# A third shuffle buffer, attention products 28 chunks behind the scores, and the gate product behind later halves

## The chip, the cores and the metric

The kernel runs on one core of a Trainium2 chip. The metric is the device time of one execution in microseconds (us). Five engines run their own instruction streams in order and wait for each other by semaphores: TensorE (PE, matmuls; its weight loads are listed as PEld), VectorE (DVE), ScalarE (ACT), GpSimd (POOL) and SyncE (SP), which here issues every DMA.

## What is computed

One block of a diffusion backbone: a modulated RMS norm, one input projection, then two parallel branches (latent attention with 4 heads, and a multi-scale pooling), gates, an output projection and the residual. The change touches the attention alone. Cut to it:

```python
def _attend(q, k, v):                     # 4 heads, 2048 queries, 2304 keys
    s = einsum('bhqd,bhkd->bhqk', q, k) * scale
    p = softmax(s, axis=-1)
    return einsum('bhqk,bhkd->bhqd', p, v)

def _branches(u, mla_out, w_pool, pool_scale):
    br_a = silu(gate_a) * mla_out          # the gate that the change moves
    br_p = silu(gate_p) * _multiscale_pool(...)
    return concatenate([br_a, br_p], -1)
```

The kernel attends in the space of the 128 compressed values ("latents") and applies each head's value matrix afterwards; numerators are normalised only at the end, by the reciprocal sums of the softmax folded into the gate.

## The kernel before

The first 520 us hold the projections. Attention runs from about 520 to 1086 us, and the output projection from there to the end. The change lies in the attention.

**Tiling.** There are 16 blocks of 512 queries (4 heads by 4), and each block is two pairs of 128-query tiles; `p` counts the pairs, 0 to 31, and `i` the tile in a pair. The keys come in chunks: four of 512 columns and one of 256 for each tile, so a pair has 10 chunks (`PER`). Chunk 4 or 9 of a pair is the narrow one.

**Scores.** `scores(p, i)` makes a chunk with 5 fp16 matmuls (L772), takes its maximum on DVE (L775), and, once the five maxima of a tile are there, their bias on DVE (L780, L781). Then ACT takes the five exponentials (L793), and DVE transposes each in 32x32 blocks into a W buffer (L796). Wide chunks use the five PSUM banks pA, narrow ones the two banks pX. The pX banks also serve `norm` (L876) and `finish` (L903).

**Shuffle.** `shuffle(p)` moves the pair's transposed numerators with 16 DMAs (L811) from its transpose buffer (two, by p % 2) to a shuffled buffer (two, by p % 2), so that keys lie on partitions.

**Products with the latents.** `pv(p)` takes nine steps. Each step splits 512 shuffled columns into two fp16 halves, the high half on ACT (L853) and the low half on POOL, for step 4 on DVE (L855); then 6 matmuls (L821) add into one PSUM bank pO, two with the high half first, then four for which the low half must be there. Three buffers hold halves, so the halves of a step wait for the matmuls three steps back. One bank pO serves a block (two pairs); when it is full, `latents` splits it into two parts (ACT L96, DVE L97), and only then can the next block write pO.

**Gate.** `norm(n)` makes the reciprocal sums of a block (DVE L873, L874), turns them on PE (L876), copies them (DVE L878), sends them to DRAM (SP L879, L881), reads them back on all partitions (L884), loads the gate (L886), and multiplies both on POOL (L887). `finish` multiplies the latents by the head's value matrix (PE L903) and by the gate (DVE L905) and stores the result (SP L908).

**Order.** `attn` yields chunk by chunk and draws steps of `pv_all` by `while done < (gc - LAG) * 9 / PER`, with `LAG = 22` chunks. A list scheduler then fixes each engine's instruction order at compile time from these priorities, so an instruction can stand some places from where the source has it. `K_PF` loads the next head's keys behind pairs 3 and 5 of a head (L712), and `WO_PF` loads output weights behind pairs 28 to 30.

Of the kernel before, what the change touches and what calls it, by code (L numbers as in the profile page):

```python
# [12 lines left out]
ALU = mybir.AluOpType  # L13
# [39 lines left out]
ATT_MAX = 18  # L53


LAG = 22
K_PF = (3, 5)
WO_AT = (1, 5, 11, 12, 12, 12, 13, 13)
CHUNKS = ((0, 512), (512, 512), (1024, 512), (1536, 512), (2048, 256))
# [4 lines left out]
def tile_hybrid_block(ctx: ExitStack, tc: tile.TileContext, x, c, cx, c_ctx, w_mod, b_mod, norm_g,  # L64
                      w_in, q_lora_g, w_uq, kv_lora_g, w_ukv, q_norm_g, k_norm_g, w_pool,
                      pool_scale, w_out, rope_t, edge_t, out):
    nc = tc.nc
    x, cx, out = x[0], cx[0], out[0]
# [671 lines left out]
    tbuf, pbuf = [], []  # L740
# [57 lines left out]
        RS.setdefault(p // 2, []).append(rs)  # L798
        yield

    PT = {}

    def shuffle(p):

        src = TP.pop(p)
        if p < 2:
            pbuf.append(st("W", [4, 2, NJ, 32]))
        dst = pbuf[p % 2]
        for iq in range(4):
            for jq in range(4):  # L810
                last = nc.sync.dma_start(out=dst[32 * jq:32 * jq + 32, iq], in_=src[32 * iq:32 * iq + 32, jq])  # L811
        PT[p] = dst
        return last.ins
# [31 lines left out]
    def pv(p):  # L845
        o = out_bank(p)
        src = PT.pop(p).rearrange("p q i j b -> p (q i) j b")
        ts = []

        def halves(j2):  # L850
            t = st("M", [2, 2, 8, 32], F16)
            s2 = src[:, :, 2 * j2:2 * j2 + 2, :].rearrange("p x j b -> p j x b")
            nc.scalar.activation(out=t[:, 0], in_=s2, func=AF.Copy)  # L853
            eng = nc.vector if j2 == 4 or (p == NP - 2 and j2 % 2) else nc.gpsimd
            eng.tensor_tensor(out=t[:, 1], in0=s2, in1=t[:, 0], op=ALU.subtract)  # L855
            ts.append(t)

        for j2 in range(NJ // 2):
            if j2 == 0:
                halves(0)  # L860
                halves(1)
            if j2 + 2 < NJ // 2:
                halves(j2 + 2)
            t = ts.pop(0)
            pv_mm(p, o, j2, t)
            yield

    def norm(n):

        h, qb = blocks[n]  # L870
        s4 = small(4, "s4")
        for i in range(4):
            nc.vector.reduce_sum(s4[:, i:i + 1], RS[n][i], axis=AX.X)  # L873
        nc.vector.reciprocal(out=s4, in_=s4)  # L874
        b = pt("X")
        nc.tensor.transpose(b[0:4, 0:128], s4, ident)  # L876
        rr = sm.tile([4, 128], F32, tag="rr", bufs=2, name=nm("rr"))
        nc.vector.tensor_copy(out=rr, in_=b[0:4, 0:128])  # L878
        nc.sync.dma_start(out=rvd[n].rearrange("(s n i r) -> s i n r", s=2, n=4, i=2)[0],  # L879
                          in_=rr[0:2].rearrange("i (n r) -> i n r", n=4))  # L880
        nc.sync.dma_start(out=rvd[n].rearrange("(s n i r) -> s i n r", s=2, n=4, i=2)[1],  # L881
                          in_=rr[2:4].rearrange("i (n r) -> i n r", n=4))
        rb = st("T", [512])
        nc.sync.dma_start(out=rb, in_=rvd[n].partition_broadcast(128))  # L884
        ga = st("T", [512])
        nc.sync.dma_start(out=ga, in_=gad[h, :, qb * 512:(qb + 1) * 512])  # L886
        nc.gpsimd.tensor_tensor(out=ga.rearrange("p (r n) -> p r n", n=16),  # L887
                                in0=ga.rearrange("p (r n) -> p r n", n=16),
                                in1=rb.rearrange("p (n r) -> p r n", n=16), op=ALU.mult)
        return ga  # L890

    def latents(n):

        o = O.pop(n)
        ol = [st("T", [512], F32R) for _ in range(2)]
        split(o, *ol)
        return ol
# [31 lines left out]
    def pv_all():  # L929
        ol = None  # L930
        for p in range(NP - 2):
            if p % 2:
                gau = norm(p // 2)
            for k, _ in enumerate(pv(p)):
                if k == 2 and ol:
                    finish(p // 2 - 1, ol, gaus)
                    ol = None
                yield
            if p % 2:
                ol, gaus = latents(p // 2), gau  # L940
        gau = norm(NP // 2 - 1)
        for k, _ in enumerate(pv_last(NP - 1)):
            if k == 2:
                finish(NP // 2 - 2, ol, gaus)
            yield
        yield from pv(NP - 2)
        finish(NP // 2 - 1, latents(NP // 2 - 1), gau)

    PER = 10
# [3 lines left out]
    def attn():  # L953

        done = 0
        for p in range(NP):
            if p % 2 == 0 and p // 2 + 1 < len(blocks):
                load_q(blocks[p // 2 + 1])
            gc = p * PER
            h = p // 8 + 1  # L960
            for i in range(2):
                for _ in scores(p, i):
                    gc += 1
                    while done < (gc - LAG) * 9 / PER:
                        next(pg)
                        done += 1
                    yield
            if p == NP - 1:
                load_wo(3)
                return  # L970
            with tc.issue_after(shuffle(p)):
                if h < H and p % 8 in K_PF:
                    load_k(h, (K_PF.index(p % 8),))
                if p in WO_PF:
                    load_wo(WO_PF.index(p))
# [129 lines left out]
```

## Time and profile before

| | before |
|---|---|
| times of 3 runs | 1288.63, 1289.40 (median), 1295.37 us |
| the profiled execution | 1288.46 us, of which the span from first to last instruction is 1286.7 us |
| PE busy | 1212.8 us (94%) |
| DVE, ACT, POOL busy | 831.1 (65%), 738.5 (57%), 562.1 us (44%) |
| PE busy in 560 to 1086 us | 495.5 of 526 us |
| DVE, ACT, POOL busy in 560 to 1086 us | 422.6, 383.5, 300.9 us |
| mean granted TensorE clock | 0.984 of full speed |

"Busy" is the time in which an engine had an instruction running. A busy PE is not a PE at its peak: at the lower of its two clocks (1.2 instead of 2.4 GHz) the same matmuls are busy for twice as long. Times inside the profile count from the first instruction. The profile's time lies 0.94 us under the median of the runs.

### The profile page before, as it was taken

What the parts mean: (1) busy time and instruction counts of PE and PEld (TensorE: products, weight loads), DVE (VectorE), ACT (ScalarE), POOL (GpSimd) and SP (SyncE); (2) the same over time, 40 slices, a digit from 0 to 9 for tenths busy, and PEclk for the clock granted to TensorE, in tenths of its full rate; (3) what the DMA queues carried; (4) which work ended last, traced back from release to release, by engine and by line L of the source; (5) the groups of instructions that cost most, each with busy time, mean ns of one, the idle gap of its engine ahead of it and who ended that gap; (6) DMA issues with size and microseconds to landing.
All of it is one profiled execution on the core that took longest, in us unless ns stands there. A gap on an engine that the chain in (4) does not pass through costs nothing.

```text
span 1286.7 us, 22292 instructions
## 1 busy us (share of the span) xinstructions
PE 1212.8 (94%) x7805; PEld 954.5 (74%) x7805; DVE 831.1 (65%) x1595; ACT 738.5 (57%) x1780; POOL 562.1 (44%) x638
## 2 busy tenths in 40 slices
PE   6799999999999998988999989999899999899998
PEld 3698989989899998755566655666556667688887
DVE  4966654765666555677788887888778887631211
ACT  5575665655575654466777767777667777511000
POOL 3645313524344342025566645654656654332221
PEclk9799999999999999999999999999999999999999
DMA  9446952574446547367877787777777778563321
GB/s 304 149 122 138 228 137 66 130 198 136 94 108 153 113 126 196 90 150 172 199 188 181 182 203 188 182 176 196 185 176 183 179 191 236 194 238 135 115 98 49
DMA packets 208213, 208.66 MB, mean 162 GB/s; under 512 B 92339, under 2 KB 168420, under 8 KB 207974
## 3 DMA queue, kind: packets, MB, share of 16 engines
q1 hardware_dynamic: 208102, 207.25, 62.0%
q8 instruction: 61, 1.00, 0.3%
q14 instruction: 50, 0.41, 0.1%
HBM read 98.50 MB, written 35.56 MB: 104 GB/s over the span
## 4 chain that ended last, share of the span: by engine, by line
PE 70%; DMA 11%; DVE 5%; SPq 5%; ACT 4%; issue 2%; POOL 2%; ACTq 0%; DVEq 0%; POOLq 0%
PE pA L588 17%; PE pA L1028 14%; PE pA L772 14%; PE pO L821 9%; PE pA L244 6%; SPq L811 3%; PE pA L519 2%; POOL M L855 2%; DMA M<-in_w_in_dram 2%; DMA rvd<-rr 2%; ACT M L853 2%; PE pX L772 1%; DMA W<-W 1%; DVE W L796 1%; PE pA L494 1%
## 5 line engine op out<-in xcount | busy, mean ns | idle before, releaser
L855 POOL TENSOR_TENSOR M<-W,M 128x512 f16<-128x512 f32 x244 | 291.3, 1218 | 193.3 <-ACT M L853 193.2
L772 PE MATMUL pA<-B,M 128*128 128x512 f16 x1280 | 303.9, 381 | 7.0 <-ACT T L793 3.6
L588 PE MATMUL pA<-W,B 128*128 128x256 f32 x2304 | 307.3, 287 | 0.1
L588 PEld LDWEIGHTS pA<-W,B 128*128 128x128 f32 x2304 | 290.2, 192 | 3.5 <-issue 0.9
L772 PEld LDWEIGHTS <-M 128*128 128x128 f16 x1600 | 156.4, 98 | 145.6 <-issue 7.3
L821 PE MATMUL pO<-M,B 128*128 128x256 f16 x1728 | 222.1, 276 | 21.2 <-POOL M L855 20.3
L793 ACT ACTIVATE T<-pA,nm,gm 128x512 f32<-128x512 f32 x248 | 189.6, 775 | 62.7 <-DVE nm L781 62.7
L821 PEld LDWEIGHTS <-B 128*128 128x128 f16 x1728 | 168.9, 99 | 71.6 <-issue 31.6
L796 DVE STREAM_TRANSPOSE W<-T 128x512 f32<-128x512 f32 x310 | 197.6, 647 | 25.2 <-ACT T L793 14.3
L853 ACT ACTIVATE M<-W 128x512 f16<-128x512 f32 x279 | 164.7, 632 | 84.3 <-PE pO L821 65.2
L775 DVE TENSOR_REDUCE mx<-pA 128x1 f32<-128x512 f32 x256 | 173.3, 680 | 37.8 <-PE pA L772 36.3
L1028 PE MATMUL pA<-W,B 128*128 128x512 f32 (+1 forms) x792 | 178.7, 386 | 4.8 <-ACT B L96 4.8
L1028 PEld LDWEIGHTS pA<-W,B 128*128 128x128 f32 x792 | 146.0, 189 | 34.2 <-ACT B L96 5.1
L1052 POOL TENSOR_TENSOR M<-T,M 128x512 f32<-128x512 f32 x30 | 38.7, 1294 | 113.6 <-DVE T L1049 109.4
L1049 DVE TENSOR_TENSOR T<-pA,M 128x512 f32<-128x512 f32 (+1 forms) x33 | 22.0, 673 | 101.1 <-PE pA L1028 101.1
L244 PE MATMUL pA<-B,W 128*128 128x448 f32 (+1 forms) x288 | 86.4, 371 | 0.0
L97 DVE TENSOR_TENSOR B<-M,B 128x1024 fp32r<-128x1024 f32 x48 | 61.5, 1282 | 32.1 <-ACT B L96 32.0
L96 ACT ACTIVATE B<-M 128x1024 fp32r<-128x1024 f32 (+2 forms) x53 | 55.3, 1044 | 45.2 <-DMA M<-in_w_in_dram 37.5
L887 POOL TENSOR_TENSOR T<-T,T 128x512 f32<-128x512 f32 x16 | 24.6, 1540 | 82.8 <-DMA T<-gad 49.5
L96 ACT ACTIVATE B<-B 128x2048 fp32r<-128x2048 f32 x8 | 15.3, 1918 | 75.2 <-DMA B<-brd 75.2
L244 PEld LDWEIGHTS pA<-B,W 128*128 128x128 f32 x288 | 54.7, 197 | 4.4 <-DVE T L275 0.9
L244 PE MATMUL pA<-W,W 128*128 128x448 f32 (+1 forms) x144 | 52.9, 369 | 0.0
(193 smaller groups left out, 1513.4 us busy)
## 6 DMA issues: line engine op xcount, KB each, us to landing
W<-W SPq DMA_DIRECT2D x496, 144.0 KB
M<-in_w_in_dram SPq DMA_DIRECT2D x48, 512.0 KB
B<-in_x_dram SPq DMA_DIRECT2D x16, 512.0 KB
B<-brd SPq DMA_DIRECT2D x8, 1024.0 KB
M<-in_x_dram SPq DMA_DIRECT2D x16, 512.0 KB
out_dram<-M SPq DMA_DIRECT2D x15, 512.0 KB
brd<-T SPq DMA_DIRECT2D x24, 256.0 KB
kd<-T SPq DMA_DIRECT2D x36, 128.0 KB
```

Source lines behind the costliest of these rows:

```text
L96: a = nc.scalar.activation(out=hi, in_=src, func=AF.Copy)
L97: (eng or nc.vector).tensor_tensor(out=lo, in0=src, in1=hi if hi.dtype == F16 else hi.bitcast(F32), op=ALU.subtract)
L244: nc.tensor.matmul(p[:, c0:NTOK], lhsT=a[:, kt, k * 128:(k + 1) * 128], rhs=b, start=(kt == 0 and n == 0), stop=(kt == KT - 1 and n == 2))
L588: nc.tensor.matmul(p[:, i * HB:(i + 1) * HB], lhsT=w[:, a, kt, :], rhs=b[:, kt, :], start=(m == 0), stop=(m == 23))
L772: nc.tensor.matmul(b[:, s0:s0 + sn], lhsT=q[:, a, c, p % 2, i], rhs=kt[ki][:, kc, o:o + sn], start=(m == 0), stop=(m == 4))
L775: nc.vector.reduce_max(mx[:, n:n + 1], b[:, :w], axis=AX.X)
L793: nc.scalar.activation(out=e[:, :w], in_=sp[n][:, :w], func=AF.Exp, bias=ng, scale=escale, accum_out=rs[:, n:n + 1])
L796: nc.vector.transpose(TP[p][:, :, i, j0:j1, :].rearrange("p q j b -> p j q b"), e[:, :w].rearrange("p (j q b) -> p j q b", q=4, b=32))
L821: nc.tensor.matmul(o, lhsT=V[0][:, j, a], rhs=t[:, c, jj], start=(j == 0 and m == 0), stop=(j == NJ - 1 and m == 2))
L853: nc.scalar.activation(out=t[:, 0], in_=s2, func=AF.Copy)
L855: eng.tensor_tensor(out=t[:, 1], in0=s2, in1=t[:, 0], op=ALU.subtract)
L1028: nc.tensor.matmul(bank[k, n, c0][:, 0:c1 - c0], lhsT=a[:, kt, k * 128:(k + 1) * 128], rhs=w[:, c, kt % 2, n * 512 + c0:n * 512 + c1], sta ...
```

## The change

A third shuffled buffer is taken, so that `shuffle(p)` uses buffer p % 3. `LAG` becomes 28, and falls in the last pairs, from chunk 280 on, by one for every four chunks to 22. `norm` no longer issues the gate product: it returns the two loaded tiles, and a new `gate_norm` issues the product just before `finish`, which moves from after step 2 to after step 3 of the next pair. An ordering edge without a semaphore puts the product behind the last low half on POOL that has been issued in the source by then (at that point the low half of step 5, since halves are made two steps ahead). In the last pair the product comes between `pv_last` and `pv`.

```diff
-LAG = 22
+LAG = 28
+
+LAG_END, LAG_LAST = 28, 22
...
-        if p < 2:
+        if p < 3:
             pbuf.append(st("W", [4, 2, NJ, 32]))
-        dst = pbuf[p % 2]
+        dst = pbuf[p % 3]
...
-            eng.tensor_tensor(out=t[:, 1], in0=s2, in1=t[:, 0], op=ALU.subtract)
+            lo = eng.tensor_tensor(out=t[:, 1], in0=s2, in1=t[:, 0], op=ALU.subtract)
+            if eng is nc.gpsimd:
+                pool_last.append(lo.ins)
...
-        nc.gpsimd.tensor_tensor(out=ga.rearrange("p (r n) -> p r n", n=16),
-                                in0=ga.rearrange("p (r n) -> p r n", n=16),
-                                in1=rb.rearrange("p (n r) -> p r n", n=16), op=ALU.mult)
+        return ga, rb
+
+    def gate_norm(ga, rb):
+
+        m = nc.gpsimd.tensor_tensor(out=ga.rearrange("p (r n) -> p r n", n=16),
+                                    in0=ga.rearrange("p (r n) -> p r n", n=16),
+                                    in1=rb.rearrange("p (n r) -> p r n", n=16), op=ALU.mult)
+        order(pool_last[-1], m.ins, "the halves come first")
         return ga
...
             if p % 2:
-                gau = norm(p // 2)
+                gr_ = norm(p // 2)
             for k, _ in enumerate(pv(p)):
-                if k == 2 and ol:
-                    finish(p // 2 - 1, ol, gaus)
+                if k == 3 and ol:
+                    finish(p // 2 - 1, ol, gate_norm(*gaus))
                     ol = None
                 yield
...
         for k, _ in enumerate(pv_last(NP - 1)):
-            if k == 2:
-                finish(NP // 2 - 2, ol, gaus)
+            if k == 3:
+                finish(NP // 2 - 2, ol, gate_norm(*gaus))
             yield
+        gau = gate_norm(*gr_)
         yield from pv(NP - 2)
...
-                    while done < (gc - LAG) * 9 / PER:
+                    lag = LAG - max(0, min(LAG - LAG_LAST, (gc - LAG_END * PER) / 4))
+                    while done < (gc - lag) * 9 / PER:
```

The built programs show what the scheduler made of it. On POOL, in the middle of the attention, before: the low halves of one pair (read from buffer W_6733), the gate product, then the low halves of the next pair (W_6927).

```order
L855 TENSOR_TENSOR M_10645<-W_6733,M_10645 128x512
L855 TENSOR_TENSOR M_10661<-W_6733,M_10661 128x512
L855 TENSOR_TENSOR M_10677<-W_6733,M_10677 128x512
L887 TENSOR_TENSOR T_10776<-T_10776,T_10774 128x512
L855 TENSOR_TENSOR M_10779<-W_6927,M_10779 128x512
L855 TENSOR_TENSOR M_10782<-W_6927,M_10782 128x512
L855 TENSOR_TENSOR M_10785<-W_6927,M_10785 128x512
```

In the changed kernel the line of the low halves is L857 and that of the product L895. The product stands inside an even pair, after five of its eight POOL halves:

```order
L857 TENSOR_TENSOR M_11059<-W_6733,M_11059 128x512
L857 TENSOR_TENSOR M_11062<-W_6733,M_11062 128x512
L857 TENSOR_TENSOR M_11065<-W_6733,M_11065 128x512
L857 TENSOR_TENSOR M_11100<-W_6733,M_11100 128x512
L857 TENSOR_TENSOR M_11149<-W_6733,M_11149 128x512
L895 TENSOR_TENSOR T_10839<-T_10839,T_10837 128x512
L857 TENSOR_TENSOR M_11173<-W_6733,M_11173 128x512
L857 TENSOR_TENSOR M_11189<-W_6733,M_11189 128x512
```

So the product has moved some ten halves back, and it now comes only a few instructions ahead of the `finish` that uses it.

On DVE, at that `finish`, before: the bias of the tile (L780, L781) and the split of pO (L97) come first, then `finish`'s multiplication L905, whose gate product was made half a block earlier.

```order
L780 TENSOR_REDUCE nm_11035<-mx_10964 128x1
L781 TENSOR_SCALAR nm_11035<-nm_11035,gm 128x1
L775 TENSOR_REDUCE mx_11070<-pA_11071 128x1
L97 TENSOR_TENSOR T_10993<-pO_10547,T_10992 128x512
L796 STREAM_TRANSPOSE W_6457<-T_11039 128x4x4x32
L796 STREAM_TRANSPOSE W_6457<-T_11042 128x4x4x32
L905 TENSOR_TENSOR T_11067<-pX_11063,T_10776 128x512
```

In the changed kernel the same multiplication is L914, the maxima are L777, the bias L782 and L783, the copy of the turned sums L882:

```order
L857 TENSOR_TENSOR M_11133<-W_6733,M_11133 128x512
L777 TENSOR_REDUCE mx_11125<-pA_11166 128x1
L777 TENSOR_REDUCE mx_11125<-pA_11182 128x1
L777 TENSOR_REDUCE mx_11233<-pA_11234 128x1
L777 TENSOR_REDUCE mx_11125<-pX_11198 128x1
L914 TENSOR_TENSOR T_11163<-pX_11159,T_10839 128x512
L782 TENSOR_REDUCE nm_11205<-mx_11125 128x1
L783 TENSOR_SCALAR nm_11205<-nm_11205,gm 128x1
L882 COPY rr_11282<-pX_11280 4x128
```

The multiplication, which reads the product T_10839 above, now stands ahead of the next tile's bias, and the copy L882 behind that.

On SP, around the keys that are loaded for the next head (L712), before: two shuffles in a block, the round trip of the sums (L879 to L886) between them.

```order
L881 DMA rvd<-rr_10770 2x4x32
L884 DMA T_10774<-rvd 128x512
L886 DMA T_10776<-gad 128x512
L811 DMA W_6733<-W_6457 32x1152 x16
L735 DMA M_10960<-qd 128x1024
L737 DMA M_10960<-qrd 64x1024 x2
L811 DMA W_6927<-W_6750 32x1152 x16
L712 DMA B_10958<-kd 128x3x1536
L908 DMA brd<-T_11067 128x512
```

In the changed kernel (shuffle L813, round trip L883 to L890, queries L737 and L739, keys L714):

```order
L885 DMA rvd<-rr_10833 2x4x32
L888 DMA T_10837<-rvd 128x512
L890 DMA T_10839<-gad 128x512
L737 DMA M_10909<-qd 128x1024
L739 DMA M_10909<-qrd 64x1024 x2
L813 DMA W_6927<-W_6750 32x1152 x16
L714 DMA B_10907<-kd 128x3x1536
L813 DMA W_7083<-W_6457 32x1152 x16
L917 DMA brd<-T_11163 128x512
```

Three shuffled buffers (W_6733, W_6927, W_7083) take turns, and the second shuffle no longer waits behind a round trip that begins after the keys.

## Rows read from the trace of the kernel before

**Rows 1.** The page: span and number of instructions.

```profile
span 1286.7 us, 22292 instructions
```

**Rows 2.** Waits: engine line <- what ended them: us in total, times, longest.

```profile
POOL T L887 <- DMA T<-gad: 49.5, 10, 9.6
POOL T L887 <- DMA W<-W: 33.4, 6, 7.9
PE pO L821 <- POOL M L855: 20.3, 14, 4.1
```

**Rows 3.** Timeline of PE at `finish`: start us, us, engine, line, [idle before <- releaser].

```profile
603.04 0.73 PE L903 MATMUL pX<-T,M 128*128 128x512 f32 x2 [0.69 <-ACT T L96]
...
845.60 0.74 PE L903 MATMUL pX<-T,M 128*128 128x512 f32 x2 [0.69 <-ACT T L96]
878.77 0.74 PE L903 MATMUL pX<-T,M 128*128 128x512 f32 x2 [0.69 <-ACT T L96]
...
1055.65 0.72 PE L903 MATMUL pX<-T,M 128*128 128x512 f32 x2 [0.69 <-ACT T L96]
```

**Rows 4.** Timeline of PE: two of the products that waited for low halves.

```profile
585.65 0.82 PE L821 MATMUL pO<-M,B 128*128 128x256 f16 x6 [4.05 <-POOL M L855]
...
764.95 2.72 PE L821 MATMUL pO<-M,B 128*128 128x256 f16 x12 [3.84 <-POOL M L855]
```

**Rows 5.** Timeline of SP, ACT and POOL ahead of the second of these.

```profile
750.20 0.28 SPq L881 DMA_DIRECT2D rvd<-rr  x1
...
756.35 0.38 SPq L886 DMA_DIRECT2D T<-gad  x1
...
756.84 12.46 SPq L811 DMA_DIRECT2D W<-W  x16
...
757.21 1.68 ACT L853 ACTIVATE M<-W 128x512 f16<-128x512 f32 x3
...
762.26 1.52 POOL L887 TENSOR_TENSOR T<-T,T 128x512 f32<-128x512 f32 x1 [7.90 <-DMA W<-W]
```

**Rows 6.** Windows: start:end, us, busy us (instructions) by engine, granted clock, DMA, GB/s.

```profile
845.60:878.77 33.17, 32.48 (x212) 20.85 (x212) 27.96 (x59) 25.24 (x60) 20.46 (x18) 1.00 0.77 184
738.61:777.20 38.59, 34.06 (x213) 21.44 (x213) 28.50 (x59) 25.58 (x60) 20.07 (x18) 0.96 0.77 188
580.00:600.00 20.00, 15.95 (x93) 9.57 (x92) 13.54 (x30) 12.16 (x29) 10.14 (x9) 0.91 0.69 168
```

**Rows 7.** The page's groups: count | busy us, mean ns of one | idle before, releaser.

```profile
L855 POOL TENSOR_TENSOR M<-W,M 128x512 f16<-128x512 f32 x244 | 291.3, 1218 | 193.3 <-ACT M L853 193.2
L793 ACT ACTIVATE T<-pA,nm,gm 128x512 f32<-128x512 f32 x248 | 189.6, 775 | 62.7 <-DVE nm L781 62.7
L796 DVE STREAM_TRANSPOSE W<-T 128x512 f32<-128x512 f32 x310 | 197.6, 647 | 25.2 <-ACT T L793 14.3
L775 DVE TENSOR_REDUCE mx<-pA 128x1 f32<-128x512 f32 x256 | 173.3, 680 | 37.8 <-PE pA L772 36.3
```

**Rows 8.** Chain of waits: start us, us, 18 product and 20 score matmuls unbroken.

```profile
720.88 1.97 PE pO L821 x18
722.85 4.32 PE pA L772 x20
```

**Rows 9.** Timeline of a block without a wait: `finish`, the turned sums, their copy.

```profile
848.26 0.65 DVE L905 TENSOR_TENSOR T<-pX,T 128x512 f32<-128x512 f32 x1
...
853.62 0.27 PE L876 MATMUL pX<-ident,s 128*4 128x128 f32 x1
...
854.43 0.27 DVE L878 COPY rr<-pX 4x128 f32<-4x128 f32 x1
```

**Rows 10.** Timeline: the low half on DVE alone, and beside POOL's halves.

```profile
872.11 0.68 DVE L855 TENSOR_TENSOR M<-W,M 128x512 f16<-128x512 f32 x1
...
1043.14 6.81 POOL L855 TENSOR_TENSOR M<-W,M 128x512 f16<-128x512 f32 x6
...
1048.99 1.52 DVE L855 TENSOR_TENSOR M<-W,M 128x512 f16<-128x512 f32 x1
```

More of the change, by code (lines that the diff above doesn't have):

```diff
@@ L799, in scores @@
         yield
-    PT = {}
+    PT, pool_last = {}, []
     def shuffle(p):
         src = TP.pop(p)
-        if p < 2:
+        if p < 3:
             pbuf.append(st("W", [4, 2, NJ, 32]))
-        dst = pbuf[p % 2]
+        dst = pbuf[p % 3]
         for iq in range(4):
@@ L939, in pv_all @@
             if p % 2:
-                ol, gaus = latents(p // 2), gau
-        gau = norm(NP // 2 - 1)
+                ol, gaus = latents(p // 2), gr_
+        gr_ = norm(NP // 2 - 1)
         for k, _ in enumerate(pv_last(NP - 1)):
-            if k == 2:
-                finish(NP // 2 - 2, ol, gaus)
+            if k == 3:
+                finish(NP // 2 - 2, ol, gate_norm(*gaus))
             yield
+        gau = gate_norm(*gr_)
         yield from pv(NP - 2)
```

## The prediction

> **What bounds the kernel now.** I read the waits first, then PE's timeline at `finish`, then the windows. PE is busy nearly throughout the attention, and the three rows with POOL or DMA in the list of waits are one story [rows 2]: the gate product L887 stands in POOL's fixed order and waits 49.5 us for its gate tile and 33.4 us for shuffled data, 82.9 us in all. That is idle time of an engine that has time to spare, and costs only where somebody waits for POOL: PE does for 20.3 us, 14 times, at the products that need low halves.
>
> The timeline at `finish` gives the price with what follows from it [rows 3]. A plain block takes 878.77 - 845.60 = 33.17 us. From the first to the last row shown there are 13 blocks, 1055.65 - 603.04 = 452.61 us, and 13 x 33.17 = 431.21, so 21.4 us are lost against a stretch without disturbance. The windows say what these are [rows 6]. The plain block has PE busy for 32.48 of 33.17 us at clock 1.00 (the 2.4 GHz level): PE is the bound, and its 0.69 us of idle are one wait, for ACT's part of the split of pO [rows 3]. A block with a key load takes 38.59 us. Of the 5.42 us more, 3.84 are one stall before a product [rows 4], and the other 1.58 are more busy time at a mean clock of 0.96, since PE after a pause is granted the lower level for a while.
>
> The cause of that stall is in the rows ahead of it [rows 5]. SP issues the turned sums at 750.20, and the load of the gate at 756.35, behind the round trip. The shuffle (756.84, 12.46 us of issuing) follows in the same queue. Shuffled data for the next pair are there (ACT starts high halves at 757.21), but POOL can't make the low halves that belong to them: L887 is ahead in its order, is idle for 7.90 us and starts at 762.26. PE runs dry at 764.95 - 3.84 = 761.1, and gets its first low half 2.7 us after L887 starts: 1.52 for the product, 1.22 for a half [rows 5, 7].
>
> **What the change takes away.** The product moves some ten low halves back, and comes just ahead of the `finish` that needs it. Ten halves are more than half a block, over 16 us, and L887's longest wait was 9.6 [rows 2]: the tiles are there when POOL comes to it. The half next to it needs no wait either. With the third buffer and six more chunks of distance, the second shuffle of a block no longer stands behind the round trip: it can be issued before it, and what PE takes from it comes about 27 us later instead of about 20 (estimate: six chunks are 6/20 of a block's 33.17 us, 10 us, less what the shuffle waits for its buffer). So I take back the whole excess: 21.4 us, and the stall ahead of the first row, 4.05 us at 585.65 [rows 4], with the lower clock behind it (0.91 over 20 us, 20 x 0.09 = 1.8 [rows 6]). Together 21.4 + 5.8 = **27.2 us**. If the cover is gone, in blocks with keys to load, part of it stays (rival 2).
>
> **What it adds at the start and the end.** Distance 28 instead of 22 makes six more chunks run before the first product. They are work that is done anyway, but ACT and DVE have to supply them without product steps between: a wide chunk has 1.08 us on PE (20 matmuls in 4.32 us [rows 8]), against 0.775 on ACT and 0.68 + 0.65 on DVE [rows 7], so DVE is behind by up to 0.25 a chunk, 1.5 us, and with the two biases some 2.2. Between 0 and 2.2 I take **1 us**. At the end the distance is taken back to 22, and the last pairs come in the order of before: nothing, except that the last product stands behind `pv_last`, beside PE's nine steps.
>
> **What it adds in each block.** This is the term that decides. `finish` used to find its gate product made half a block ago. Now the product is the middle of a chain POOL, DVE, PE, DVE, PE within a few us: the fifth low half, the product (1.52 [rows 5]), the multiplication by the gate (0.65), the turn of the sums in the same pX bank (0.27), its copy (0.27) [rows 9], then the narrow score chunk, which wants that bank. I laid the order of the changed program against these durations, from PE's first `finish` matmul at T = 0.
>
> Place A: from T = 0 PE has `finish` itself (two matmuls at 0.73 [rows 3]), five score chunks (four wide at 1.08 and a narrow one at 0.54, 4.9 us) and six product steps (6 x 6 x 0.11, 4.0 us [rows 8]), 10.3 us without a wait, and it gets to the narrow chunk at T = 10.3 to 10.6. POOL has its fifth half at T = 7.1 (the third buffer of halves comes free by step 2, and five halves of 1.22 follow from just before T = 0). Then 1.52 gives 8.6, 0.65 gives 9.3. On DVE the bias of the tile now stands behind this multiplication instead of ahead; the turn on PE and the copy, behind the bias, are ready at T = 10.5 to 10.85. The exposed part is **0 to 0.5 us**.
>
> Place B, half a block later: step 8 of the pair releases the halves that ACT and DVE queue behind. Tile 2 of the next pair has its exponentials only behind the high half of step 3, about T = 18.4. DVE then has five transposes (0.65), maxima (0.68) and the low half of step 4 (0.68 alone, 1.52 beside POOL's halves [rows 7, 10]) in a row ahead of the bias that ACT's first exponential needs. It ends at T = 28.2, and PE arrives at 27.4: **0.5 to 0.9 us**.
>
> Place C: DVE's part of the split of pO (L97) stands behind a maximum and a bias, about **0.3 us**, in which the existing 0.69 us of wait grows.
>
> Together 0.8 to 1.7 a block, taken at 1.4, in 12 blocks: 16.8 us. The bounds are 0 (DVE is busy for 27.96 of 33.17 us [rows 6], so it has 5.2 us to absorb this) and 2.7 (the product's chain 1.52 + 0.65 + 0.27 + 0.27 wholly exposed). I take a value in the middle because the two waits of DVE have rows beside them, but their places are worked out by hand to some 0.5 us.
>
> The sum is made against the profiled execution, 1288.46 us with a span of 1286.7 [rows 1] and 1.8 around it: 1288.46 - 27.2 + 1 + 16.8 = 1279.1. It lies 0.94 under the median of the runs of 1289.4, which I don't correct for.
>
> One row speaks more sharply against the change: a low half on DVE takes 0.68 us alone and 1.52 beside POOL's run of halves [rows 10], 0.84 more. Moving the product moves what POOL does while DVE makes `finish`'s multiplication and low halves. The Trainium skill, "SBUF — State Buffer", section "Who interferes with whom", says that a DVE instruction with two SBUF inputs contends with a GpSimd instruction that reads SBUF, and that the one which starts first shuts the other out until it is done. By the rule a low half of DVE that meets the gate product could wait for all of its 1.52 us; by the row it waits for 0.84. In place B that is 0.7 us a block more, 8 us in 12 blocks, so 1287 by the rule against 1279. The row agrees with the kind of the effect; it doesn't show the full block.
>
> **The rivals.** Rival 1, *no new idle*: DVE's 5.2 us of slack take up the new places, as they take up the one wait that a plain block shows. Then 1288.46 - 27.2 + 1 = **1262** (1258 to 1266, from the start's 0 to 2.2 and the clock). For it: PE is the bound with 32.48 of 33.17, and its queue of scores runs ahead. Against it: the narrow chunk has only two banks, shared with `finish` and the sums, and the order puts the bias behind the multiplication.
>
> Rival 2, *the queue is full in blocks with keys*: SP needs about 33 us in such a block (two shuffles of 12.46 and some 11, the round trip from 750.20 to 756.35 [rows 5], about 3 of others), as long as the block itself, so that the shuffle is late and PE still stalls, 9 us less recovered: **1288**. For it: DMA is busy for 0.77 of the block [rows 6]. Against it: the plain block has the same 0.77 and no stall, and by the third buffer there are some 10 us to spare.
>
> Rival 3, *slower*: POOL's fifth half ends no earlier than PE comes to its product, so the gate's chain is wholly exposed: 2.7 us in each of 14 blocks, 38 us, and 1288.46 - 27.2 + 1 + 38 = **1300**. It decides from 2.4 us a block on (1296). For it: POOL's low halves are what PE waits for now [rows 2]. Against it: POOL is busy for 20.46 of 33.17 us [rows 6], and 5 halves come ahead.
>
> Rival 4, *the change doesn't do what it says*: the scheduler keeps the old distance. Then **1288**. The order on POOL and SP speaks against it; only the waits on buffers could undo it.
>
> **How the numbers follow.** The forecast, 1279 (own range 1270 to 1287, for 0.7 to 2.1 us a block), has a chance of 0.48; rival 1 0.27, rival 2 0.12, rival 3 0.08, rival 4 0.05. A measurement of this kernel can tell about 0.5%, 6.4 us, so faster is under 1283.0 and slower over 1295.8. Faster: rival 1 and three quarters of the forecast, 0.27 + 0.36 = 0.63. Slower: rival 3, 0.08. Within: 0.29. The range takes in rivals 1, 2 and 4 and the forecast, without rival 3 and the low part of rival 1: 1260 to 1290.
>
> **What would show it.** Right: POOL's waits for the gate and the shuffle, 82.9 us, nearly gone; PE's wait for low halves, 20.3, under 8; the distance between `finish` rows even, 34 to 35 us, also with keys loaded; new idle time of PE of 0.2 to 0.9 us before the narrow chunk (ended by DVE's copy of the turned sums) and before scores (ended by ACT's exponential); the clock at 0.99 or more. The step "no new idle" is right instead if the distance is 33.2 (rival 1). The queue is full if blocks with keys are still longer than plain ones (rival 2), and the chain is exposed if all take over 35.5 (rival 3). The forecast is wrong in either direction if the places by hand are off by half a microsecond, which is 6 us in 12 blocks.

## The result and the profile after

The changed kernel takes 1266.8 us (median of 4 runs, 1264.59 to 1268.39) against 1289.78 us (1288.63 to 1295.37) for the kernel before: a ratio of 0.9827, interval 0.9802 to 0.9852. On another chip it was 0.9871, interval 0.9846 to 0.9896 (e8 below). It is faster by some 1.3 to 1.7%, and lies 12 us under the forecast of 1279.

In the changed kernel the lines of the attention have moved: PE's products are L823, its scores L774, its `finish` matmuls L912, the turned sums L880, ACT's exponentials L795 and high halves L855, and the splits L98 and L99.

The waits of the changed kernel (engine, line <- what ended them: us in total, times, longest) against [rows 2]:

```profile
POOL M L857 <- DMA W<-W: 21.9, 7, 3.4
POOL T L895 <- DMA T<-gad: 15.9, 1, 15.9
PE pX L912 <- ACT T L98: 9.5, 14, 0.7
```

Of the 82.9 us that the gate product waited for data one wait is left, 15.9 us in the last block. POOL's low halves now wait for shuffled data themselves, but PE hardly feels it: the page's row of its products (count | busy us, mean ns | idle before, releaser) has 1.8 us of waiting for low halves, against 20.3 before.

```profile
L823 PE MATMUL pO<-M,B 128*128 128x256 f16 x1728 | 219.7, 273 | 3.0 <-POOL M L857 1.8
```

PE's timeline at `finish`, of a stretch with key loads, answers [rows 3]:

```profile
735.80 0.73 PE L912 MATMUL pX<-T,M 128*128 128x512 f32 x2 [0.69 <-ACT T L98]
769.64 0.73 PE L912 MATMUL pX<-T,M 128*128 128x512 f32 x2 [0.69 <-ACT T L98]
803.48 0.74 PE L912 MATMUL pX<-T,M 128*128 128x512 f32 x2 [0.69 <-ACT T L98]
837.32 0.74 PE L912 MATMUL pX<-T,M 128*128 128x512 f32 x2 [0.69 <-ACT T L98]
871.16 0.73 PE L912 MATMUL pX<-T,M 128*128 128x512 f32 x2 [0.69 <-ACT T L98]
```

The distance is 33.84 us from row to row, with keys and without: the stalls are gone from the blocks. Between the second and the thirteenth `finish` all eleven distances lie between 33.83 and 33.85. But a plain block of before took 33.17 [rows 3], so 0.67 us are new in each. The first of the thirteen distances is 34.44, and the last, where `LAG` falls to 22 and fewer score chunks stand between two `finish`, is 28.86. The window of one block (start:end, us, busy us and instructions of PE, PEld, DVE, ACT, POOL, clock, DMA share, GB/s) answers [rows 6]:

```profile
837.32:871.16 33.84, 32.80 (x212) 20.81 (x213) 28.42 (x59) 24.99 (x60) 20.46 (x18) 1.00 0.78 178
```

PE is idle for 1.04 us of it instead of 0.69, and 0.32 us more busy with the same 212 matmuls at the same clock. Its timeline shows two waits that were not there, here in the block from 769.64:

```profile
779.51 0.38 PE L823 MATMUL pO<-M,B 128*128 128x256 f16 x2
780.05 0.71 PE L774 MATMUL pX<-B,M 128*128 128x256 f16 x5 [0.15 <-DVE rr L882]
...
794.68 2.35 PE L823 MATMUL pO<-M,B 128*128 128x256 f16 x20
797.23 1.24 PE L774 MATMUL pA<-B,M 128*128 128x512 f16 x5 [0.20 <-ACT T L795]
```

The first is place A of the prediction, the second place B. The chain of place A shows on DVE too, where the multiplication of `finish` waits for the product:

```profile
778.53 0.69 DVE L914 TENSOR_TENSOR T<-pX,T 128x512 f32<-128x512 f32 x1 [0.41 <-POOL T L895]
```

A wait costs more than its brackets say. Two matmuls of L823 start 0.1094 us apart (18 in 1.97 us [rows 8]), so without a wait the narrow chunk would have started at 779.51 + 0.22 = 779.73; it starts at 780.05, 0.32 later. The other would have started at 794.68 + 20 x 0.1094 = 796.87, and starts at 797.23, 0.36 later. In either case this is 0.16 to 0.17 us more than the bracket: a row of 20 matmuls ends 2.35 us after its start, 0.16 after a next one would have started, and this overlap is lost when the stream breaks. 0.32 + 0.36 = 0.68: that is the whole of the 0.67.

The span fell from 1286.7 to 1264.2, by 22.5 us. Two stretches can be compared as they are, since PE issues the same matmuls in both kernels: from the bias of the first tile to the fourteenth `finish`, and from there to the end. Windows (columns as above), before:

```profile
524.81:1055.65 530.84, 496.20 (x3173) 316.20 (x3172) 424.91 (x876) 377.16 (x877) 285.92 (x241) 0.99 0.73 176
1055.65:1286.70 231.05, 220.81 (x1125) 178.78 (x1125) 84.98 (x111) 56.26 (x91) 68.36 (x51) 0.99 0.48 154
```

and after:

```profile
523.10:1035.37 512.27, 491.95 (x3172) 313.40 (x3170) 425.76 (x876) 373.10 (x877) 286.42 (x241) 1.00 0.76 183
1035.37:1264.20 228.83, 220.81 (x1125) 177.24 (x1125) 85.25 (x111) 55.90 (x91) 70.65 (x51) 1.00 0.48 153
```

The first stretch is 18.6 us shorter. The forecast's 27.2 less, 11 x 0.67 = 7.4 more and 1.3 more in the first block (34.44 against 33.17, with a wait of 0.95 us of the turned sums for DVE's bias) give 18.5. The second is 2.2 us shorter, all of it idle time of PE. The other 1.7 us stand before the attention: the first tile's bias comes at 523.10 instead of 524.81, in code that the change doesn't touch. Over all the runs it comes between 522.9 and 527.0, so this part isn't shown to come from the change.

In the tail the largest difference is the wait ahead of PE's first matmul of the output projection, 3.2 us less; shorter waits around it take 1.0 us back. Three rows follow each other there: SP issues the load of the projection's input (B<-brd), ACT waits for it and splits it, and PE waits for ACT. Before, the timelines of SP, ACT and PE:

```profile
1086.01 0.80 SPq L1017 DMA_DIRECT2D B<-brd  x1
```
```profile
1097.12 1.91 ACT L96 ACTIVATE B<-B 128x2048 fp32r<-128x2048 f32 x1 [5.77 <-DMA B<-brd]
```
```profile
1099.09 3.61 PE L1028 MATMUL pA<-W,B 128*128 128x512 f32 x8 [4.84 <-ACT B L96]
```

and the same three after:

```profile
1063.79 0.50 SPq L1028 DMA_DIRECT2D B<-brd  x1
```
```profile
1073.93 1.91 ACT L98 ACTIVATE B<-B 128x2048 fp32r<-128x2048 f32 x1 [3.02 <-DMA B<-brd]
```
```profile
1075.90 1.21 PE L1039 MATMUL pA<-W,B 128*128 128x512 f32 x4 [1.65 <-ACT B L98]
```

PE runs dry at 1099.09 - 4.84 = 1094.25 before and at 1074.25 after. The load is issued 8.2 us ahead of that before and 10.5 us after, and from its issue to ACT's start it takes 11.1 us before and 10.1 after: 2.2 + 1.0 = 3.2, the difference of the two waits. In both kernels SP issues it behind the last shuffle; 2.2 us of the gain are work that PE still has at that point. How long PE waits there differs from run to run: in e8, the changed kernel once more, it is 0.64 us.

### The profile page after: what moved, and what is told of

It is laid out like the page before. It is cut to its first block, busy times and chain, and to the rows that moved or that the text cites. A ratio compares the mean times of both kernels' runs of the same rounds, so it can differ in the third digit from the quotient of the medians.

```text
span 1264.2 us, 22297 instructions
## 1 busy us (share of the span) xinstructions
PE 1208.2 (96%) x7805; PEld 949.8 (75%) x7805; DVE 832.2 (66%) x1595; ACT 733.5 (58%) x1780; POOL 565.7 (45%) x638
## 4 chain that ended last, share of the span: by engine, by line
PE 75%; DMA 9%; DVE 6%; ACT 5%; SPq 3%; issue 2%; POOL 1%; ACTq 0%; DVEq 0%; POOLq 0%
PE pA L590 17%; PE pA L774 17%; PE pA L1039 13%; PE pO L823 10%; PE pA L246 6%; DMA W<-W 2%; PE pA L521 2%; PE pX L774 2%; ACT T L795 2%; DVE W L798 2%; DMA M<-in_w_in_dram 2%; SPq L813 1%; PE pX L912 1%; DVE mx L777 1%; DMA qrd<-U 1%
## 5 line engine op out<-in xcount | busy, mean ns | idle before, releaser
L857 POOL TENSOR_TENSOR M<-W,M 128x512 f16<-128x512 f32 x244 | 291.5, 1219 | 239.1 <-ACT M L855 187.7
L774 PE MATMUL pA<-B,M 128*128 128x512 f16 x1280 | 298.1, 379 | 8.5 <-ACT T L795 6.1
L774 PEld LDWEIGHTS <-M 128*128 128x128 f16 x1600 | 154.7, 98 | 153.3 <-issue 13.9
L798 DVE STREAM_TRANSPOSE W<-T 128x512 f32<-128x512 f32 x310 | 194.1, 643 | 58.5 <-ACT T L795 44.6
L855 ACT ACTIVATE M<-W 128x512 f16<-128x512 f32 x279 | 162.2, 633 | 107.6 <-PE pO L823 95.0
L823 PE MATMUL pO<-M,B 128*128 128x256 f16 x1728 | 219.7, 273 | 3.0 <-POOL M L857 1.8
L823 PEld LDWEIGHTS <-B 128*128 128x128 f16 x1728 | 167.6, 98 | 48.1 <-issue 11.2
L795 ACT ACTIVATE T<-pA,nm,gm 128x512 f32<-128x512 f32 x248 | 189.3, 773 | 7.8 <-DVE nm L783 6.3
L777 DVE TENSOR_REDUCE mx<-pA 128x1 f32<-128x512 f32 x256 | 168.3, 671 | 11.5 <-PE pA L774 11.2
L98 ACT ACTIVATE B<-M 128x1024 fp32r<-128x1024 f32 (+2 forms) x53 | 55.2, 1043 | 43.3 <-DMA M<-in_w_in_dram 37.4
L99 DVE TENSOR_TENSOR B<-M,B 128x1024 fp32r<-128x1024 f32 x48 | 59.8, 1247 | 30.9 <-ACT B L98 30.9
L98 ACT ACTIVATE B<-B 128x2048 fp32r<-128x2048 f32 x8 | 15.3, 1914 | 77.4 <-DMA B<-brd 77.4
L246 PEld LDWEIGHTS pA<-B,W 128*128 128x128 f32 x288 | 54.7, 197 | 4.4 <-DVE T L275 0.9
L795 ACT ACTIVATION_READ_ACCUMULATOR T<-pA,nm,gm 128x1 f32 x248 | 49.5, 200 | 0.0
```

What stands on the lines that cost most here:

```text
L98: a = nc.scalar.activation(out=hi, in_=src, func=AF.Copy)
L99: (eng or nc.vector).tensor_tensor(out=lo, in0=src, in1=hi if hi.dtype == F16 else hi.bitcast(F32), op=ALU.subtract)
L246: nc.tensor.matmul(p[:, c0:NTOK], lhsT=a[:, kt, k * 128:(k + 1) * 128], rhs=b, start=(kt == 0 and n == 0), stop=(kt == KT - 1 and n == 2))
L774: nc.tensor.matmul(b[:, s0:s0 + sn], lhsT=q[:, a, c, p % 2, i], rhs=kt[ki][:, kc, o:o + sn], start=(m == 0), stop=(m == 4))
L777: nc.vector.reduce_max(mx[:, n:n + 1], b[:, :w], axis=AX.X)
L795: nc.scalar.activation(out=e[:, :w], in_=sp[n][:, :w], func=AF.Exp, bias=ng, scale=escale, accum_out=rs[:, n:n + 1])
```

## The experiments

All are timed against the kernel before on the same chip. "Block" is the distance of two `finish` rows in the undisturbed middle of the attention.

| | time, us | ratio (interval) | block, us |
|---|---|---|---|
| before | 1285 to 1292 | | 33.17, with keys to 38.6 |
| e1 product alone | 1268.4 | 0.9833 (0.9790 to 0.9877) | 33.48, four of 33.8 to 35.6 |
| e2 distance and buffer alone | 1286.1 | 0.9982 (0.9956 to 1.0007) | 33.3 to 35.4 |
| e3 two buffers | 1567.5 | 1.2164 (1.2115 to 1.2213) | 54.7 to 56.5 |
| e4 distance 22 | 1262.5 | 0.9793 (0.9748 to 0.9839) | 33.48 |
| e5 product two halves earlier | 1260.2 | 0.9758 (0.9721 to 0.9795) | 32.76 |
| e6 low half on POOL | 1269.5 | 0.9833 (0.9799 to 0.9868) | 33.75 |
| e7 both | 1261.5 | 0.9773 (0.9731 to 0.9814) | 33.00 |
| e8 changed kernel again | 1269.3 | 0.9871 (0.9846 to 0.9896) | 33.84 |
| e9 early product, distance 22 | 1264.4 | 0.9834 (0.9810 to 0.9858) | 33.28 |
| e10 e9, last product late | 1261.7 | 0.9815 (0.9791 to 0.9839) | 33.28 |
| e11 e9, two buffers | 1265.9 | 0.9849 (0.9821 to 0.9878) | 33.28 |

Runs e1 to e4 were on one chip, e5 to e7 on another, e8 to e11 on a third. Ratios of different groups differ by some 0.4% for the same kernel (0.9827 and 0.9871 for the changed one), so that only blocks, and times inside a group, are compared below.

**Which part brought the gain.** The change has two parts: the product's place, and the distance with its buffer. e1 and e2 each do one. (In e1 the reduction of the distance at the end stays in the code, and has no effect at 22.)

```diff
 e1 (against the changed kernel; the product stays late)
-LAG = 28
+LAG = 22
...
-        if p < 3:
+        if p < 2:
-        dst = pbuf[p % 3]
+        dst = pbuf[p % 2]
```

> Edit: the kernel before with only the gate product moved (behind the last low half issued, finish after step 3); distance 22, two shuffled buffers. Theory 1 (the product's place in POOL's order alone made PE's stalls in the blocks with key loads): PE's waits for low halves fall from 20.3 us to under 6, the distance between finish rows is even at 33.8 us as in the changed kernel, and the time is 1266 to 1272. Theory 2 (the stalls went because the third buffer and the distance bring shuffled data earlier): blocks with keys stay longer than plain ones by 2 us or more, and the time is 1280 to 1296.

```diff
 e2 (against the changed kernel; the product as before)
-                gr_ = norm(p // 2)
+                gr_ = (gate_norm(*norm(p // 2)),)
...
-        order(pool_last[-1], m.ins, "the halves come first")
...
-                if k == 3 and ol:
-                    finish(p // 2 - 1, ol, gate_norm(*gaus))
+                if k == 2 and ol:
+                    finish(p // 2 - 1, ol, *gaus)
...
```

> Edit: distance 28 with its reduction at the end and three shuffled buffers, but the gate product issued in norm, and finish after step 2, as in the kernel before. Theory 1: POOL still waits for the gate tile ahead of the next pair's low halves, PE's stalls stay in part, time 1280 to 1290. Theory 2: no stalls, no new waits either (no chain product to finish), 33.2 us a block, time 1256 to 1266.

The product alone takes 1268.4 us, the distance and the buffer alone 1286.1, the kernel before 1288.5 on this chip. The waits of e2 say why:

```profile
POOL T L895 <- DMA T<-gad: 40.1, 10, 10.6
PE pO L823 <- POOL M L857: 25.9, 41, 5.6
```

POOL waits for the gate tile as before [rows 2], and PE for low halves in 41 places instead of 14. Six chunks of distance and a third buffer make the stalls more frequent and on average shorter (0.6 against 1.5 us), and don't take them away. Theory 1 holds: the place of the product in POOL's order is the cause, and the whole gain, within the intervals, comes with it. e1 moves `finish` by one step together with the product; the later `finish` was not tried alone.

e4 keeps the third buffer and the late product, and sets the distance back:

```diff
-LAG = 28
+LAG = 22
```

> Edit: the changed kernel with the distance at 22 throughout (third buffer and moved product kept). Theory 1: the same as the product alone, within 2 us, 1266 to 1272, as the distance gives nothing of itself. Theory 2: stalls come back in blocks with keys, 1276 or more. The start of the attention and the tail are those of before: if the tail's 3 us gain comes from the distance, it is missing here.

It has no stalls, and 33.48 us a block instead of 33.84; its 1262.5 us are less than either theory has. Its timeline has the wait of place A and not that of place B:

```profile
774.89 0.27 PE L880 MATMUL pX<-ident,s 128*4 128x128 f32 x1
775.00 0.38 PE L823 MATMUL pO<-M,B 128*128 128x256 f16 x2
775.53 0.71 PE L774 MATMUL pX<-B,M 128*128 128x256 f16 x5 [0.15 <-DVE rr L882]
...
791.69 1.24 PE L774 MATMUL pA<-B,M 128*128 128x512 f16 x5
792.77 0.60 PE L823 MATMUL pO<-M,B 128*128 128x256 f16 x4
```

With the product as late as in the change, place B is the distance's own price, 0.36 us a block. The tail's first projection matmul waits for 1.24 us here, so the gain in the tail doesn't come from the distance either. e1, without the third buffer, has blocks of 35.64, 35.13, 33.78 and 34.23 us among its 33.48. e4 has one longer block, the first, of 35.22, so that e1 loses 3.1 us in blocks; by the medians it is 5.9 us slower (the intervals overlap). Three of e1's four, like e4's one, have PE waiting longer for the split of pO, because ACT has the split behind high halves that wait for a DMA in blocks with key loads:

```profile
632.76 1.15 ACT L855 ACTIVATE M<-W 128x512 f16<-128x512 f32 x2 [3.79 <-DMA M<-qd]
633.82 0.58 ACT L98 ACTIVATE T<-pO 128x512 fp32r<-128x512 f32 x1
```
```profile
634.45 0.72 PE L912 MATMUL pX<-T,M 128*128 128x512 f32 x2 [1.95 <-ACT T L98]
```

The block of 35.13 stands behind the wait of 1.95 us. It has no long wait itself, but a mean granted clock of 0.95, where e1's plain blocks have 1.00:

```profile
634.45:669.58 35.13, 34.30 (x212) 21.48 (x212) 27.89 (x59) 24.99 (x60) 21.11 (x19) 0.95 0.75 185
```

e3 was to say whether the distance needs the third buffer.

```diff
-        if p < 3:
+        if p < 2:
-        dst = pbuf[p % 3]
+        dst = pbuf[p % 2]
```

> Edit: the changed kernel with two shuffled buffers instead of three (distance 28 kept). If the third buffer is what the distance needs: a shuffle waits for low halves of two pairs back, which come six chunks (10 us) later than at distance 22, transposes wait for their buffer, exponentials behind them, and a block takes 35 us or more, time 1280 or more. If it is spare: 33.8 us a block and 1266.

It answers another question. At a distance of 28 chunks the source issues the shuffle of pair p ahead of the last steps of pair p - 2, which with two buffers are the same tile: these steps then read the numerators of pair p, and have to wait for them. The part of the computation that changes is these steps' operand. PE's wait is then not for a free buffer:

```profile
PE pO L823 <- ACT M L855: 217.4, 28, 11.1
```

So the third buffer isn't a matter of speed at a distance of 28: without it another thing is computed. How long a shuffle would wait for a free buffer at this distance no run shows.

**Whether the two waits are the 0.67 us.** e5 puts the product two halves earlier, behind the third of the pair:

```diff
-        order(pool_last[-1], m.ins, "the halves come first")
+        order(pool_last[-3], m.ins, "the halves come first")
```

> Edit: the changed kernel, but the gate product stands behind the third low half of the pair instead of the fifth, in the time in which POOL waits for a high half anyway. If the 0.67 us that a block has more than before are PE's two new waits (0.15 us ahead of the narrow chunk, ended by the copy of the turned sums, and 0.20 ahead of a wide one, ended by an exponential, each with some 0.16 us of a refilled pipeline): the first is gone, 33.5 us a block, 4 us less than the changed kernel in 13 blocks. If the 0.67 are something else (another order on PE, DMA traffic): 33.84 stays.

The block is 32.76 us, better than expected, and less than the plain block of before. PE's timeline:

```profile
772.72 0.27 PE L880 MATMUL pX<-ident,s 128*4 128x128 f32 x1
772.83 2.13 PE L823 MATMUL pO<-M,B 128*128 128x256 f16 x18
774.80 0.71 PE L774 MATMUL pX<-B,M 128*128 128x256 f16 x5
...
785.69 0.82 PE L823 MATMUL pO<-M,B 128*128 128x256 f16 x6 [0.34 <-POOL M L857]
...
792.95 4.48 PE L774 MATMUL pA<-B,M 128*128 128x512 f16 x20
797.08 0.82 PE L912 MATMUL pX<-T,M 128*128 128x512 f32 x2
```

The wait of place A is gone, as expected. So are place B and the 0.69 us ahead of `finish`, which was not expected: with the product elsewhere, the scheduler's list comes out otherwise, and PE has four score chunks between the last product of a block and its `finish`, which cover the split of pO. A wait of 0.34 us for a low half is new. By the brackets and 0.16 each: 33.84 - 0.32 - 0.36 - 0.85 + 0.50 = 32.81, against 32.76. e7 and e6 move DVE's low half to POOL, with and without the earlier product:

```diff
-            eng = nc.vector if j2 == 4 or (p == NP - 2 and j2 % 2) else nc.gpsimd
+            eng = nc.vector if (p == NP - 2 and j2 % 2) else nc.gpsimd
```

> Edit: the changed kernel, but the low half of step 4 is made on POOL, not on DVE (POOL 1.2 us more a pair, DVE 1.2 to 1.3 less). The second wait (0.20 us) is gone, as DVE's low half takes 1.3 us beside POOL where it takes 0.68 alone, and is in the chain to the bias. But the gate product comes one half later: the wait ahead of the narrow chunk grows from 0.15 to 0.8 to 1.3 us. Sum a block: 34.1 to 34.8 us, 1268 to 1278. If POOL's extra half is hidden: 33.5.

> Edit: both, the gate product behind the third low half and the low half of step 4 on POOL. If the two waits are the whole of the 0.67 us: 33.17 us a block as in the plain block of the kernel before, 8.7 us less than the changed kernel, some 1258. If POOL becomes the bound in the second half of a pair: more than 33.5 us a block, with PE waiting for low halves.

e6: place B is gone, and the turned sums now wait for DVE's multiplication, because the product comes a half later:

```profile
848.95 0.27 PE L880 MATMUL pX<-ident,s 128*4 128x128 f32 x1 [0.24 <-DVE T L914]
```

33.75 us a block, less than the 34.1 to 34.8 expected, since the scheduler has moved the narrow chunk away from behind the turn. e7: 33.00 us. POOL has room for the half, but it doesn't beat e5, which leaves it on DVE. So for the changed kernel the theory of two waits holds, by the sum of its own rows (0.68 of 0.67) and by e4 (the wait of place B gone, 0.36 less, with that of place A still there). For e5 to e7 it is only a part, since PE's order changes as well.

**What is best.** e8 to e11 ran together.

> The changed kernel itself, beside the three below on the same chip: 33.84 us a block, 1264 to 1269.

> Edit: the changed kernel with the gate product behind the third low half and the distance at 22. If the six chunks of distance cost a wait of their own (33.84 against 33.48 us a block, 0.36, with the product late): 32.4 us a block and 1252 to 1256. If this wait was one of the late product alone, which is gone with the early one: 32.8 us a block and 1256 to 1262.

> Edit: as e9_early_distance_22, but in the last pair the product stays behind the latest low half, as in the changed kernel. If the tail's order on PE decides its 3 to 4 us (PE waits 5.65 us for the first split of the output projection's input with the early product, 1.65 with the late one): 2 to 4 us less than e9_early_distance_22. If not: the same.

> Edit: the kernel before with the product alone moved, behind the third low half: distance 22, two shuffled buffers. If the third buffer is worth nothing of itself: as e9_early_distance_22 within 2 us. If blocks with keys need it (e1_product_alone had 35.6, 35.1 and 34.2 us in three blocks, e4_distance_22 33.5 in all but the first): 3 to 5 us more.

```diff
 e9 (against the changed kernel)
-LAG = 28
+LAG = 22
-        order(pool_last[-1], m.ins, "the halves come first")
+        order(pool_last[-3], m.ins, "the halves come first")
 e10: as e9, but pool_last[-1] in the last pairs (the products of the last two blocks)
 e11: as e9, with two shuffled buffers
```

e9 fits neither expectation: 33.28 us a block, 0.52 more than e5 with its distance of 28. The largest part is in one row of its timeline:

```profile
732.87 0.73 PE L912 MATMUL pX<-T,M 128*128 128x512 f32 x2 [0.69 <-ACT T L98]
```

The 0.69 us ahead of `finish` are back, worth 0.85 with the break, while the 0.50 of e5's wait for a low half is gone; the rest of the 0.52 was not followed. So the distance of 28 does pay, if the product is early: it has score chunks at hand where PE would wait for the split. With the late product it costs 0.36 a block instead.

e10 is 2.7 us faster than e9, within the 2 to 4 expected. Their intervals overlap by 0.0029 in the ratio, but every run of e10 is below every run of e9 (1262.86 us at most against 1262.87 at least), and from the fourteenth `finish`, at 1032.39 and 1030.71, to the end the profiles differ by 2.8 us. So in the tail the late product is better, but not for the reason in the expectation, the wait of 5.65 us that e5 has. In e9 PE begins the projection without a wait, and loses its time in shorter ones, the longest behind that:

```profile
1072.78 1.17 PE L1039 MATMUL pA<-W,B 128*128 128x512 f32 x4
...
1095.30 0.81 PE L823 MATMUL pO<-M,B 128*128 128x256 f16 x6 [1.80 <-POOL M L857]
```

The longest in e10's tail is 1.23 us. e11 is as e9 within 1.5 us, and the intervals overlap widely, so that no worth of the third buffer with the early product is shown; its runs spread from 1261.1 to 1273.4 us.

By the medians all three are faster than the changed kernel beside them (1269.3): by 4.9, 7.6 and 3.4 us. For e9 and e10 every run is below every run of e8; for e11 the runs and the intervals overlap, and the difference isn't shown. e5 has the shortest blocks, and in its tail PE waits 5.65 us ahead of the projection. No run joins e5's blocks to e10's tail.

## Why the prediction was wrong, step by step

- *What bounds the kernel, and the cause of the stalls*: right. The product in POOL's order made PE wait, and where it stands alone decides (e1 against e2).
- *What the change takes away, 27.2 us*: right in size, as the blocks are even and the stretch up to the fourteenth `finish` is 18.6 us shorter with 8.6 us of new waits in it. Its reason was half wrong: I gave a part of it to the distance and the third buffer, which of themselves bring 0.2% in e2, by an interval that reaches no change.
- *The start, 1 us*: not found. -27.2 and the new waits make up the stretch without it, but it can't be told apart from the first stall that went. PE's waits in the first 40 us of the attention are those of before, but for one of 0.93 us that is 0.15 now.
- *The end, nothing*: wrong, by 2.2 us, with 3.2 in one wait. I compared the order of the tail on each queue and found the same, and didn't work out how long before PE's last attention step the projection's load is issued. That was 8.2 us for a load of 11.1, so a few us of PE's work placed otherwise decide a wait.
- *What it adds in each block, 1.4 us*: the step that failed. The mechanism was right and the size was not: it is 0.67, so 7.4 us in eleven blocks and 1.3 in the first, 8.6 instead of 16.8 in 12. Of the 0.73 too much in a block, place C gives 0.30, place B 0.34 and the choice of 1.4, where the middle of 0.8 to 1.7 is 1.25, gives 0.15; place A takes 0.07 back. The 0.16 us that a break costs beyond its idle time were not in my sum, or the places would have come out larger still. Place A was right: 0 to 0.5 expected, 0.32 measured, with PE arriving at T = 10.26 (780.05 - 0.15 - 769.64). That PE's arrival came out was luck: [rows 3] gives 0.73 us for both `finish` matmuls together, where my 10.3 needs it for each, a third matmul follows, and the products ahead of the chunk are 38, not 36, so that the terms that I named sum to 9.6 by the rows, and not to 10.3. Place B was put at 0.5 to 0.9, and is 0.36; PE's arrival was right to 0.01 us (797.23 - 0.20 - 769.64 = 27.39), ACT's exponential was 0.6 too late. DVE's rows of that place show where this is from:

```profile
791.03 0.65 DVE L777 TENSOR_REDUCE mx<-pA 128x1 f32<-128x512 f32 x1
791.61 1.02 DVE L798 STREAM_TRANSPOSE W<-T 128x512 f32<-128x512 f32 x2
792.55 0.11 DVE L877 TENSOR_REDUCE s<-rs 128x1 f32<-128x5 f32 x1
792.59 0.68 DVE L777 TENSOR_REDUCE mx<-pA 128x1 f32<-128x512 f32 x1
793.18 1.31 DVE L857 TENSOR_TENSOR M<-W,M 128x512 f16<-128x512 f32 x1
...
794.50 1.25 DVE L777 TENSOR_REDUCE mx<-pA 128x1 f32<-128x512 f32 x2
```

  I added durations, 0.65 and 0.68. A chain is worth the distances of starts: a maximum that takes 0.68 lets the next begin after 0.59 (793.18 - 792.59), one of 0.65 after 0.58, since an instruction ends while the next has begun. All of DVE's rows from 788.88 to 796.27, where the bias is ready, sum to 8.16 us in a stretch of 7.39. Place C was put at 0.3 and is 0: the wait ahead of `finish` is 0.69 in both kernels.
- *The rule on shared access*: for the wait of a low half on DVE beside POOL I had 0.84 us by the row and up to 1.52 by the rule. In place B it takes 1.31 us against 0.68 alone [rows 10], 0.63 more. The trace agrees with the rule of the Trainium skill ("SBUF — State Buffer", "Who interferes with whom") that one engine shuts the other out: beside this half, POOL's row is

```profile
792.79 2.71 POOL L857 TENSOR_TENSOR M<-W,M 128x512 f16<-128x512 f32 x2 [3.32 <-ACT M L855]
```

  where two halves take 2.27 [rows 10, 1.135 each]. DVE starts at 793.18, and POOL's first half would end at 792.79 + 1.135 = 793.92. From there DVE needs 0.57 to its end at 794.49, and POOL is 0.44 late. The other low half that DVE makes in this block comes out the same, 774.29 + 1.135 + 0.56 = 775.99:

```profile
774.77 1.22 DVE L857 TENSOR_TENSOR M<-W,M 128x512 f16<-128x512 f32 x1
```
```profile
774.29 2.72 POOL L857 TENSOR_TENSOR M<-W,M 128x512 f16<-128x512 f32 x2 [2.96 <-ACT M L855]
```

  What I got wrong was the length: in these rows the wait is for what is left of the half that is running, not for a whole instruction, and the product (1.53 from 776.97) has no DVE instruction with two inputs from SBUF beside it.
- *The chances*: rival 1, "no new idle", gave 1262, and the result lies between it and the forecast. Its mechanism didn't come true, since the two waits are there. That its number was nearer is luck: the tail and the stretch ahead of the attention gave 3.9 us that no case had, and the start cost nothing that shows (1262.3 + 8.6 - 3.9 - 1 = 1266.0). Of the forecast's signs most came: POOL's waits, PE's for low halves (1.8 us, under 8), the even distance and the clock (0.991). The two new waits are of the kinds named, but 0.15 and 0.20 us long where 0.2 to 0.9 were named, and 33.84 lies between rival 1's 33.2 and the forecast's 34 to 35. Rivals 2, 3 and 4 didn't come true.

The sum with what was measured: 1288.46 - 27.2 + 8.6 - 2.2 = 1267.7, less the 1.7 ahead of the attention 1266.0, and the profiled execution took 1265.99.

## What to carry to other kernels

An instruction on an idle engine that waits for a DMA costs what stands behind it in the same order; move it to just before its use, but a few instructions ahead of the last moment, or it becomes a link of the user's chain (late and early, 33.84 and 32.76 us a block at a distance of 28, 33.48 and 33.28 at 22). A chain worked out by hand goes by distances of starts, not by durations, and here a break in the stream of matmuls cost 0.16 us beyond its idle time. A list scheduler answers a move with another order elsewhere: e5 gained more from PE's four chunks ahead of `finish` (0.85 us) than from the wait that it was made for (0.32), so read the blocks, not only the place.

## What the runs showed of the hardware

A break in PE's stream costs 0.16 to 0.17 us more than its idle time (0.32 lost for a wait of 0.15, 0.36 for one of 0.20). DVE's maxima of 128x512 overlap by 0.07 to 0.09 us with the next instruction (0.65 and 0.58, 0.68 and 0.59 from start to start). DVE's low half and POOL's were served in turn: 1.31 us instead of 0.68 on DVE, and 2.71 for two halves instead of 2.27 on POOL.
